# Up-projection pairs in an alternating order, down activations split inside the last pair, and the last norm's weight moved to ScalarE, in a decoder block on one core

## The chip, the core and the metric

The kernel runs on one core of a Trainium2 chip. The metric is the device time of one execution in microseconds; the times given are medians over runs. The program is written against engines by name: TensorE (PE) multiplies, VectorE (DVE), ScalarE (ACT) and GpSimd (POOL) do the rest, SyncE (SP) and GpSimd issue transfers.

## The reference

One decoder block for 512 tokens of 2048 channels in float32: an RWKV-7 head group and a pooling head group that share one input projection, an output projection, then a gated feed-forward part with a causal convolution of width 3, each modulated by `c`, and a last RMS norm with weight `norm_f_g`. What matters here is the last part:

```python
def _conv_ffn(h, w_up, conv_w, conv_b, w_down):
    u = h @ w_up                                   # 2048 -> 2 * 5632
    up = jnp.pad(u, ((0, 0), (CONV_WIDTH - 1, 0), (0, 0)))
    y = conv_b
    for j in range(CONV_WIDTH):
        y = y + conv_w[j] * up[:, j:j + T]
    val, gate = jnp.split(y, 2, axis=-1)
    return (jax.nn.silu(gate) * val) @ w_down      # 5632 -> 2048
...
    mix = jnp.concatenate([y_rwkv, y_pool], axis=-1) @ w_out[l]
    x = x + gt1 * mix
    h = _rmsnorm(x, norm2_g[l]) * (1.0 + sc2) + sh2
    x = x + gt2 * _conv_ffn(h, w_up[l], conv_w[l], conv_b[l], w_down[l])
return _rmsnorm(x, norm_f_g)
```

## The kernel before

Every float32 product is made of three products of halves: a weight tile is cast by ScalarE to a high part (`uhi`, line 850) and DVE subtracts it from the weight to get the low part (`ulo`, line 852); `mm3` (lines 120 to 122) then issues three matmuls for each of the eight tiles of 128 channels. One such `product` is 24 matmuls of 256 columns (128x256 outputs). There are three buffers for `uhi` and `ulo` of the wide kind.

The up-projection runs over 44 pairs `j`; a pair is one tile of 128 value columns and one of 128 gate columns, for both halves of the tokens (`H0`, `H1`, 256 each). It uses the seven-product form for 2x2 blocks instead of eight: the right-hand sides are Y11, Y21, Y22 and sums T1, T2, T3, T4 of them, and the left-hand sides are weights and sums of weights. A pair's two rows of weights, 1 MB each (`row`, line 865), hold `w11`, `w12` in the first and `r1`, `w22` in the second. GpSimd's accumulating transfer (line 972 before) adds other weights from memory onto `r1` once that second row has landed; `r3` is loaded by SP and gets an accumulating transfer of its own (lines 974 and 975). DVE forms `r2 = r1 + w11` (line 996) and `r4 = r2 + w12` (line 1003). The products follow in the order Y11, Y21, T1, T2, Y22, T3, and the pair's last, with `w22` and T4, stands behind the next pair's first product (`last_product`). `finish_pair` then applies the convolution (two DVE passes each, lines 933 and 934, after ScalarE's), SiLU and the product with the value, and stores the activation tile to memory.

Ten pairs, `j < NB`, have their Y11 and Y21 products made earlier, in a time in which T1 to T4 are not yet there (`first_two`), and stored to memory (`early`). These are the stored pairs: in the loop they read that result back and have five products; the others, here the ordinary pairs, have seven. The row buffers of all pairs rotate through four places (`x2_0` to `x2_3`).

The engines' order is not the order of the text: a scheduler places the instructions of each engine within limits, and an engine then runs its list strictly in turn. SP's list of transfers is such a list too.

After the pairs comes the down-projection. `act_pair` loads two activation tiles (`al`), casts and splits them (lines 1040 and 1041 before); `down_four` begins four output tiles in blocks of eight activations. `ada_gate2` makes the second gate: sixteen loads of 1 MB (`wa`) and sixteen DVE dot products (`jk`, line 1027). The down weights have three wide buffers (`wd`) and two in `wd2`. At the end the residual, the rows' sums of squares, and the last norm: `finish` multiplies one tile of 128x256 by the weight and by the row's scale, and stores it.

Ahead of the pairs is the output projection, whose `out_half` splits its weights (`wlo`, line 115) on DVE, and for the last six tiles on DVE and GpSimd in turn.

Of the kernel before, what the change touches and what calls it, by code (L numbers as in the profile page):

```python
# [9 lines left out]
F32 = mybir.dt.float32  # L10
# [6 lines left out]
P = 128  # L17
# [38 lines left out]
def block_kernel(ctx, tc, a, out, stop=None, dbg=None):  # L56
# [67 lines left out]
    def project(ps, src, acts, start=True, stop=True, engs=(V,)):  # L124

        n = len(acts)
        for k0 in range(0, n, WC // P):
            wh, wl = split_weights(src[:, k0 * P : k0 * P + WC], engs[k0 // 4 % len(engs)])
            for kk in range(WC // P):
                k = k0 + kk  # L130
                sl = slice(kk * P, (kk + 1) * P)
                last = mm3(ps, wh[:, sl], wl[:, sl], *acts[k], start=start and k == 0, stop=stop and k == n - 1)
        return last
# [571 lines left out]
    def half(acts, hf):  # L705
        sl = slice(hf * HT, (hf + 1) * HT)
        return [(h[:, sl], l[:, sl]) for h, l in acts]

    def wide(name):

        return rb.tile([P, 4, HT], F32, tag="wide", name=name, bufs=3)
# [57 lines left out]
    for f in range(8):  # L769
        out_done(f, pss[f], 0, T)  # L770

    def out_half(hf, f, engs=(V,)):
        ps = bank()[:, 0:HT]
        project(ps, a["wout"][f, :, :], half(M, hf), engs=engs)
        out_done(f, ps, hf * HT, (hf + 1) * HT)


# [26 lines left out]
    for f in range(8, KT):  # L804
        if f == 9:
            dg = norm_rows(acc[:, H0])
        if f == 10:
            rstd = norm_bcast(dg)
        if f >= 10:
            next(steps, None)  # L810
            if f % 2:
                next(steps, None)
        out_half(1, f, (V, G) if f >= 10 else (V,))

    ea = ctx.enter_context(tc.tile_pool(name="ea", bufs=1, reuse_waits="tile"))
    hctx.close()
# [23 lines left out]
        def done(self):  # L840
            free.append(self.home)

    nsplit = [0]

    def wsplit(src):
        n = src.shape[-1]
        pool, tag = ((ea, "0"), (ea, "1"), (ub, "2"))[nsplit[0] % 3]
        nsplit[0] += 1
        hi = pool.tile([P, 2 * QW], F32R, tag="whi" + tag, name="uhi")
        S.copy(hi[:, 0:n], src)  # L850
        lo = pool.tile([P, 2 * QW], F32R, tag="wlo" + tag, name="ulo")
        V.tensor_tensor(lo[:, 0:n], src, hi[:, 0:n].bitcast(F32), op=ALU.subtract)  # L852
        return hi, lo

    def product(ps, w, Y, start=True):
# [82 lines left out]
    def finish_pair(j, u1, u2):  # L938
# [9 lines left out]
        nc.sync.dma_start(ad[j], yv.t)  # L948
        yv.done()

    pend = None

    def last_product(p):

        j, u1, u2, b, w22, x = p
        product(b, w22, T4, start=False)
        if x is None:
            S.copy(u2[:, H0], b)
        else:
            V.tensor_add(u2[:, H0], x[:, H0], b)  # L960
            x.done()
        finish_pair(j, u1, u2)

    rows = 0
    for j in range(NF):
        w = []
        for i in range(2):
            w.append(row(2 * j + i, rb, f"x2_{(0, 2, 1, 3)[rows % 4]}"))
            rows += 1

        w11, w12, r1, w22 = w[0][:, W1], w[0][:, W2], w[1][:, W1], w[1][:, W2]
        G.dma_start(r1, a["wup"][2 * j + 1, :, W2], accum_op=ALU.add)
        r3 = wide("r3").rearrange("p a b -> p (a b)")
        nc.sync.dma_start(r3, a["wup"][2 * j, :, W1])
        G.dma_start(r3, a["wup"][2 * j + 1, :, W1], accum_op=ALU.add)
        pa = bank()[:, 0:HT]
        cap = Slot("cap")
        if j < NB:
            u1 = Slot("u1")
            nc.sync.dma_start(u1.t, early[j])  # L980
            if pend:
                last_product(pend)
        else:
            product(pa, w11, Y11)
            S.copy(cap[:, H0], pa)
            last_product(pend)
            u1 = Slot("u1")
            pb = bank()[:, 0:HT]
            product(pb, w12, Y21)
            V.tensor_add(u1[:, H0], cap[:, H0], pb)  # L990
        u2 = Slot("u2")
        pc = bank()[:, 0:HT]
        product(pc, r1, T1)
        S.copy(cap[:, H1], pc)
        r2 = wide("r2").rearrange("p a b -> p (a b)")
        V.tensor_add(r2, r1, w11)
        product(pa, r2, T2, start=j < NB)
        if j < NB:
            V.tensor_add(cap[:, H0], u1[:, H1], pa)
        else:  # L1000
            S.copy(cap[:, H0], pa)
        r4 = wide("r4").rearrange("p a b -> p (a b)")
        V.tensor_add(r4, r2, w12)
        product(pc, r4, Y22, start=False)
        V.tensor_add(u1[:, H1], cap[:, H0], pc)
        if j < NB:
            pd = bank()[:, 0:HT]
            product(pd, r3, T3)
            V.tensor_add(u2[:, H1], cap[:, H0], cap[:, H1])
            V.tensor_add(u2[:, H1], u2[:, H1], pd)  # L1010
            pend = (j, u1, u2, pd, w22, cap)
        else:
            product(pa, r3, T3, start=False)
            V.tensor_add(u2[:, H1], cap[:, H1], pa)  # L1014
            cap.done()
            pend = (j, u1, u2, pa, w22, None)
    last_product(pend)


    cb = quad(0, "cb2").rearrange("p a b -> p (a b)")  # L1020
    nc.sync.dma_start(cb, cact[0:1, :].partition_broadcast(P))
# [2 lines left out]
    def ada_gate2(i):  # L1024
        wa = quad(1 + i % 2, "wa2").rearrange("p a b -> p (a b)")
        nc.sync.dma_start(wa, a["ada3"][i, :, :])
        V.scalar_tensor_tensor(jk, wa, 1.0, cb, op0=ALU.mult, op1=ALU.mult, accum_out=mod[:, 80 + i : 81 + i])

    ATAGS = [(rb, "y0"), (rb, "y1"), (rb, "y2"), (rb, "y3")]
    ATAGS += [(ub, f"{t}{g}") for t in ("t1", "t2", "y22", "t3") for g in range(2)] + [(ea, "t40")]  # L1030
    wd2 = ea.tile([P, 2, 2 * QW], F32, tag="t41", name="wd2")

    def act_pair(i):

        pool, tag = ATAGS[i % len(ATAGS)]
        t = pool.tile([P, 2, 2, T], F32R, tag=tag, name="act2")
        for n in range(2):
            s_ = Slot("al")
            nc.sync.dma_start(s_.t, ad[2 * i + n])
            S.copy(t[:, 0, n, :], s_.t)  # L1040
            V.tensor_tensor(t[:, 1, n, :], s_.t, t[:, 0, n, :].bitcast(F32), op=ALU.subtract)
            s_.done()
        return [(t[:, 0, n, :], t[:, 1, n, :]) for n in range(2)]

    nrow = [0]

    def down_row():
        nrow[0] += 1
        if nrow[0] % 5 < 2:
            return wd2[:, nrow[0] % 5, :]  # L1050
        return wide("wd").rearrange("p a b -> p (a b)")

    def down(ps, f, h, acts, blocks=(0, 8, 16)):
        for k0 in blocks:
# [8 lines left out]
    def down_four(h, acts):  # L1063

        pss = [bank() for _ in range(4)]
        for k0 in (0, 8, 16):
            while len(acts) < min(k0 + 8, NJ):
                acts += act_pair((h * NJ + len(acts)) // 2)
            for f in range(4):
                down(pss[f], f, h, acts, (k0,))  # L1070
        return pss

    yd = [tc.dram_tile([P, T], F32, name=f"yd{f}") for f in range(KT)]
    A, A2 = [], []
    for f in range(KT):
        if f == 0:
            pss = down_four(0, A)
        ps = pss[f] if f < 4 else bank()
        if f >= 4:
            down(ps, f, 0, A)  # L1080
        s_ = Slot("yd")
        S.copy(s_.t, ps)
        G.dma_start(yd[f], s_.t)
        s_.done()
        if f == KT - 3:
            A2 += act_pair(NJ // 2) + act_pair(NJ // 2 + 1)
        if f < 8:
            ada_gate2(2 * f)
            ada_gate2(2 * f + 1)
    V.tensor_add(mod[:, 80:96], mod[:, 80:96], cols("b_ada", 80, 96))  # L1090

    def gate(f):
# [14 lines left out]
    def down_half(hf, f):  # L1107
        ps = bank()[:, 0:HT]
        down(ps, f, 1, half(A, hf))
        residual(f, ps, gate(f), acc, hf * HT, (hf + 1) * HT, False)  # L1110

    def finish(hf, k, rstd):
        hs = slice(hf * HT, (hf + 1) * HT)
        V.scalar_tensor_tensor(x2(k, hs), x2(k, hs), col("nf", k), rstd, op0=ALU.mult, op1=ALU.mult)
        nc.sync.dma_start(out[:, k, hs], x2(k, hs))

    for f in range(NWF):
        if f == 0:
            pss = down_four(1, A)
        load_x2(f)  # L1120
        load_x2(f + NWF)
        ps = pss[f] if f < 4 else bank()
        if f >= 4:
            down(ps, f, 1, A)
        residual(f, ps, gate(f), acc, 0, T, f == 0)
    for f in range(NWF, KT):
        down_half(0, f)
    for f in range(NWF, KT):
        n = f - NWF
        if n == 1:  # L1130
            dg = norm_rows(acc[:, H0])
        if n == 2:
            rstd = norm_bcast(dg)
        for k in range(3 * (n - 2), min(3 * (n - 1), KT) if n < 7 else KT):
            if k >= 0:
                finish(0, k, rstd)
        down_half(1, f)
    rstd = norm_bcast(norm_rows(acc[:, H1]))
    for k in range(KT):
        finish(1, k, rstd)  # L1140


def pack(x, c, w_ada, b_ada, norm1_g, w_in, mu_shift, w0, w2, a0, a2, g2, k_k, k_a, r_k, ln_x_w, ln_x_b,
# [95 lines left out]
```

## Time and profile before

| | |
|---|---|
| time, median of 3 runs | 2438.1 us (2434.01 to 2439.13) |
| the profiled execution | 2440.98 us, of which the span is 2439.2 |
| mean granted TensorE clock of it | 0.985 |
| busy: TensorE, DVE, ScalarE, GpSimd | 2295.3 us (94%), 1643.0 (67%), 1039.9 (43%), 139.7 (6%) |
| moved by DMA | 483.06 MB, mean 198 GB/s |

In the rows that follow, a line such as L852 is that of the kernel before, a row "x" is a count, and times are microseconds unless marked ns. "`wrow<-wup`" names the tile written and the tensor read; buffer numbers are left out. A releaser ("<-DVE ulo L852") is the instruction that ended the wait ahead of it. The span is divided into stages: the mixers, the output projection and the second norm to about 1045 us (the output projection's last tiles from about 935 to 985), the stored pairs to 1243, the ordinary pairs to 1917, the down-projection to 2424, then the last norm.

### The profile page before, as it was taken

The numbers are of one execution on the slowest core, as the hardware profiler recorded it, in microseconds if no ns is written. First come the engines' busy times: TensorE is split into PE (matmuls) and PEld (weight loads), VectorE is DVE, ScalarE is ACT, GpSimd is POOL, SyncE is SP. The second block draws the span as 40 slices with busy tenths as digits, with TensorE's granted clock in tenths as the row PEclk, the third lists the DMA queues.
The fourth block names the chain that finished last, engine by engine and source line by source line (L and its number), as shares of the span: only waits on it lengthen the run. The fifth ranks groups of instructions, "written<-read, shape, count | busy, mean of one in ns | idle before, by whom it ended". The sixth has DMA issues, their size and how long they took to land.

```text
span 2439.2 us, 42721 instructions
## 1 busy us (share of the span) xinstructions
PE 2295.3 (94%) x17122; PEld 1986.5 (81%) x17122; DVE 1643.0 (67%) x2636; ACT 1039.9 (43%) x1466; POOL 139.7 (6%) x195
## 2 busy tenths in 40 slices
PE   4889999999999999988899999999999899999997
PEld 3656666667666898987799999999999788888897
DVE  7987777777774466866677777777777762253355
ACT  3234343443433346643345555555555522232242
POOL 0000000000000013110000000000000010010000
PEclk9999999999999999999999999999999999999999
DMA  9975565656672766677777777777676895454365
GB/s 347 343 232 154 171 172 142 168 167 178 166 206 83 245 191 181 235 217 216 218 207 200 196 199 199 201 195 199 195 196 195 282 346 179 121 195 129 112 182 164
DMA packets 214330, 483.06 MB, mean 198 GB/s; under 512 B 73521, under 2 KB 79089, under 8 KB 194673
## 3 DMA queue, kind: packets, MB, share of 16 engines
q1 hardware_dynamic: 195410, 414.77, 52.6%
q0 software_dynamic: 18720, 65.55, 13.3%
q8 instruction: 134, 2.20, 0.4%
q14 instruction: 66, 0.54, 0.1%
HBM read 441.70 MB, written 38.54 MB: 197 GB/s over the span
## 4 chain that ended last, share of the span: by engine, by line
PE 77%; DVE 9%; DMA 7%; issue 4%; ACT 3%; SPq 0%; POOL 0%; DVEq 0%; POOLq 0%; ACTq 0%
PE b L122 18%; PE b L120 18%; PE b L121 18%; PE mm L121 3%; PE mm L120 3%; PE mm L122 3%; DMA wrow<-wup 3%; DVE jk L212 2%; DVE ulo L852 1%; PE pb L537 1%; DMA war<-ada 1%; PE pb L535 1%; DMA wraw<-win 1%; PE pb L528 1%; PE pa L298 1%
## 5 line engine op out<-in xcount | busy, mean ns | idle before, releaser
L122 PE MATMUL b<-t,ulo 128*128 128x256 f32 x1408 | 404.5, 287 | 33.6 <-DVE ulo L852 33.6
L120 PE MATMUL b<-t,uhi 128*128 128x256 f32 x1408 | 402.6, 286 | 3.3 <-DVE u L1014 2.6
L121 PE MATMUL b<-t,uhi 128*128 128x256 f32 x1408 | 401.9, 285 | 0.0
L120 PE MATMUL b<-act,uhi 128*128 128x512 f32 (+1 forms) x880 | 308.5, 351 | 5.9 <-ACT uhi L850 5.9
L122 PE MATMUL b<-act,ulo 128*128 128x512 f32 (+1 forms) x880 | 308.5, 351 | 0.0
L121 PE MATMUL b<-act,uhi 128*128 128x512 f32 (+1 forms) x880 | 308.3, 350 | 0.0
L122 PEld LDWEIGHTS b<-t,ulo 128*128 128x128 f32 x1408 | 272.6, 194 | 37.1 <-DVE ulo L852 37.1
L120 PE MATMUL b<-y,uhi 128*128 128x256 f32 x1056 | 298.0, 282 | 1.3 <-ACT uhi L850 1.3
L122 PE MATMUL b<-y,ulo 128*128 128x256 f32 x1056 | 298.0, 282 | 0.4 <-DVE ulo L852 0.3
L121 PE MATMUL b<-y,uhi 128*128 128x256 f32 x1056 | 297.9, 282 | 0.0
L850 ACT CAST uhi<-wrow 128x1024 fp32r<-128x1024 f32 x176 | 183.7, 1048 | 223.0 <-PE b L121 207.0
L120 PEld LDWEIGHTS b<-t,uhi 128*128 128x128 f32 x1408 | 272.8, 194 | 4.1 <-ACT act L1040 2.8
L852 DVE TENSOR_TENSOR ulo<-wd,uhi 128x1024 fp32r<-128x1024 f32 (+1 forms) x120 | 136.1, 1135 | 205.3 <-ACT uhi L850 202.0
L121 PEld LDWEIGHTS b<-t,uhi 128*128 128x128 f32 x1408 | 272.5, 194 | 0.0
L852 DVE TENSOR_TENSOR ulo<-wrow,uhi 128x1024 fp32r<-128x1024 f32 x176 | 214.7, 1222 | 81.8 <-ACT uhi L850 81.8
L113 ACT CAST whi<-wraw 128x512 fp32r<-128x512 f32 x236 | 145.4, 618 | 286.0 <-PE mm L121 117.2
L850 ACT CAST uhi<-wd 128x1024 fp32r<-128x1024 f32 (+1 forms) x120 | 117.3, 978 | 301.4 <-PE b L121 272.3
L115 DVE TENSOR_TENSOR wlo<-wraw,whi 128x512 fp32r<-128x512 f32 x224 | 156.2, 700 | 108.0 <-ACT whi L113 92.3
L850 ACT CAST uhi<-r 128x1024 fp32r<-128x1024 f32 x132 | 138.5, 1049 | 171.0 <-PE b L121 165.5
L120 PEld LDWEIGHTS b<-y,uhi 128*128 128x128 f32 x1056 | 200.4, 190 | 1.7 <-ACT uhi L850 1.7
L122 PEld LDWEIGHTS b<-y,ulo 128*128 128x128 f32 x1056 | 199.9, 189 | 0.8 <-DVE ulo L852 0.8
L852 DVE TENSOR_TENSOR ulo<-r,uhi 128x1024 fp32r<-128x1024 f32 x132 | 160.9, 1220 | 57.9 <-ACT uhi L850 57.9
(308 smaller groups left out, 4699.3 us busy)
## 6 DMA issues: line engine op xcount, KB each, us to landing
wrow<-wup SPq DMA_DIRECT2D x98, 1024.0 KB, 5.3
wa<-ada SPq DMA_DIRECT2D x48, 1024.0 KB, 7.0
war<-ada SPq DMA_DIRECT2D x192, 256.0 KB, 3.5
wd<-wdn SPq DMA_DIRECT2D x80, 512.0 KB, 4.1
wraw<-win SPq DMA_DIRECT2D x140, 256.0 KB, 4.2
wraw<-wout SPq DMA_DIRECT2D x96, 256.0 KB, 3.6
wrow<-wup POOLq DMA_DIRECT2D x44, 512.0 KB, 5.8
r<-wup SPq DMA_DIRECT2D x44, 512.0 KB, 4.5
```

Source lines behind the costliest of these rows:

```text
L113: S.copy(hi, raw)
L115: eng.tensor_tensor(lo, raw, hi[:, :].bitcast(F32), op=ALU.subtract)
L120: PE.matmul(ps, wh, xh, start=start, stop=False, skip_group_check=more)
L121: PE.matmul(ps, wh, xl, start=False, stop=False, skip_group_check=more)
L122: return PE.matmul(ps, wl, xh, start=False, stop=stop, skip_group_check=more)
L212: V.scalar_tensor_tensor(jk, wa, 1.0, cb, op0=ALU.mult, op1=ALU.mult, accum_out=mod[:, j : j + 1])
L298: PE.matmul(ps, pw[:, i, d * P : (d + 1) * P], zs[i], start=i == 0, stop=i == 1)
L528: PE.transpose(pst[:, i * P : (i + 1) * P], src[:, cl], ident)
L535: PE.matmul(pss[h][:, 0:128], bt[HS[h], cl], ar[HS[h], c, 1, :], start=True, stop=True)
L537: PE.matmul(pss[h][:, 128:384], kt[HS[h], cl], ar[HS[h], c, :, :], start=True, stop=True)
L850: S.copy(hi[:, 0:n], src)
L852: V.tensor_tensor(lo[:, 0:n], src, hi[:, 0:n].bitcast(F32), op=ALU.subtract)
```

## The change

There are four edits. First, the 44 pairs run in the order 10, 0, 11, 1, ..., 19, 9, 20, 21, ..., 43, so that each of the ten stored pairs stands behind an ordinary one. Second, eight activation tiles of the down-projection are loaded and split by calls inside the last pair; the last pair's last product stands behind the first down product; the `ada_gate2` dot products go from output tiles 0 to 7 to tiles 4 to 11, behind the last weight split issued so far; the down weights take three wide buffers and then the two of `wd2`. Third, `out_half` splits all its weights on DVE. Fourth, the last norm's weight is multiplied in by ScalarE tile by tile as the residuals come out; `finish` then multiplies four tiles at a time by the row's scale and stores them with one transfer. For the second half of the tokens GpSimd multiplies the first four tiles, from a copy of the scale that ScalarE makes.

```diff
-    def out_half(hf, f, engs=(V,)):
+    def out_half(hf, f):
...
-        out_half(1, f, (V, G) if f >= 10 else (V,))
+        out_half(1, f)
...
+    def ahead_of_down(j):
+        if j == NF - 1:
+            A.extend(act_pair(len(A) // 2))
...
+    order = [j for n in range(NB) for j in (NB + n, n)] + list(range(2 * NB, NF))
     rows = 0
-    for j in range(NF):
+    for j in order:
...
-            last_product(pend)
+            if pend:
+                last_product(pend)
...                                 (ahead_of_down(j) after Y21, T1, T2 and Y22)
-    last_product(pend)
...
     def down_row():
+        if nrow[0] % 5 > 2:
+            w = wd2[:, nrow[0] % 5 - 3, :]
+        else:
+            w = wide("wd").rearrange("p a b -> p (a b)")
         nrow[0] += 1
-        if nrow[0] % 5 < 2:
-            return wd2[:, nrow[0] % 5, :]
-        return wide("wd").rearrange("p a b -> p (a b)")
+        return w
...
                 down(pss[f], f, h, acts, (k0,))
+                if h == 0 and k0 == 0 and f == 0:
+                    last_product(pend)
...
-        if f < 8:
-            ada_gate2(2 * f)
-            ada_gate2(2 * f + 1)
+        if 4 <= f < 12:
+            with tc.issue_after(lo_of[0].ins):
+                ada_gate2(2 * f - 8)
+                ada_gate2(2 * f - 7)
...
+    def last_residual(f, ps, lo, hi):
+        residual(f, ps, gate(f), acc, lo, hi, f == 0)
+        S.activation(x2(f, slice(lo, hi)), x2(f, slice(lo, hi)), AF.Identity, bias=eps[:, 2:3], scale=col("nf", f))
...
-    def finish(hf, k, rstd):
-        hs = slice(hf * HT, (hf + 1) * HT)
-        V.scalar_tensor_tensor(x2(k, hs), x2(k, hs), col("nf", k), rstd, op0=ALU.mult, op1=ALU.mult)
-        nc.sync.dma_start(out[:, k, hs], x2(k, hs))
+    def finish(hs, q, rstd, eng=V):
+        x = x2q[q][:, :, hs]
+        eng.tensor_tensor(x, x, rstd[:, None, :].to_broadcast([P, 4, HT]), op=ALU.mult)
+        nc.sync.dma_start(out[:, 4 * q : 4 * q + 4, hs], x)
...
-    for k in range(KT):
-        finish(1, k, rstd)
+    rs = Slot("rs")
+    S.copy(rs[:, H0], rstd)
+    finish(H1, 0, rs[:, H0], G)
+    for q in range(1, 4):
+        finish(H1, q, rstd)
```

How the order moves, at three places. SP's transfers in the stage of the stored pairs, before: the first two rows are the second row of a stored pair and the first row of the next.

```order
L865 DMA wrow_13113<-wup 128x2048
L865 DMA wrow_13343<-wup 128x2048
L974 DMA r3_13116<-wup 128x1024
L948 DMA ad11_10662<-yv_12947 128x512
L865 DMA wrow_13345<-wup 128x2048
L865 DMA wrow_13575<-wup 128x2048
L974 DMA r3_13348<-wup 128x1024
```

The same list after the change, where `u1<-early7` belongs to stored pair 7, whose rows are 13743 and 13745; the rows 13919 and 13921 are those of an ordinary pair, 14151 the first of stored pair 8.

```order
L1003 DMA u1_13753<-early7_9927 128x512
L865 DMA wrow_13745<-wup 128x2048
L865 DMA wrow_13919<-wup 128x2048
L997 DMA r3_13748<-wup 128x1024
L948 DMA ad6_10657<-yv_13579 128x512
L865 DMA wrow_14151<-wup 128x2048
L865 DMA wrow_13921<-wup 128x2048
L997 DMA r3_13924<-wup 128x1024
```

Before, a pair's second row always stood ahead of the next pair's first one. Now that holds for stored pairs, and an ordinary pair's second row (13921) stands behind the next stored pair's first one (14151).

DVE's list in the stage of the stored pairs, before. `r2_11970` belongs to the next pair, `r3_11716` and `wrow_11713` (its `w22`) to the present one.

```order
L996 TENSOR_TENSOR r2_11970<-wrow_11889,wrow_11887 128x1024
L934 SCALAR_TENSOR_TENSOR yg_11753<-u2_11587,ncw_10649,yg_11753 128x510
L852 TENSOR_TENSOR ulo_11859<-r3_11716,uhi_11857 128x1024
L946 TENSOR_TENSOR yv_11752<-yv_11752,yg_11753 128x512
L999 TENSOR_TENSOR cap_11720<-u1_11721,b_11719 128x256
L852 TENSOR_TENSOR ulo_11901<-wrow_11713,uhi_11899 128x1024
```

After: `r2_11612` belongs to an ordinary pair (rows 11471 and 11473), `r3_11300` and `wrow_11297` to the stored pair ahead of it.

```order
L1022 TENSOR_TENSOR r2_11612<-wrow_11473,wrow_11471 128x1024
L934 SCALAR_TENSOR_TENSOR yg_11337<-u2_11173,ncw_10649,yg_11337 128x510
L1025 TENSOR_TENSOR cap_11304<-u1_11305,b_11303 128x256
L852 TENSOR_TENSOR ulo_11443<-r3_11300,uhi_11441 128x1024
L946 TENSOR_TENSOR yv_11336<-yv_11336,yg_11337 128x512
L1037 TENSOR_TENSOR u2_11347<-cap_11304 128x256
L852 TENSOR_TENSOR ulo_11483<-wrow_11471,uhi_11481 128x1024
L1032 TENSOR_TENSOR u1_11305<-cap_11304,b_11348 128x256
L852 TENSOR_TENSOR ulo_11512<-wrow_11297,uhi_11510 128x1024
```

The next pair's `r2` add stands ahead of the present pair's `r3` split in both. Now the split of the ordinary pair's Y11 weight (`wrow_11471`) stands between that and the split of the stored pair's `w22`.

DVE's list at the step into the down-projection, before: `u2_20181` is the last pair's, `act2` are activations.

```order
L1041 TENSOR_TENSOR act2_20385<-al_20386,act2_20385 128x512
L1005 TENSOR_TENSOR u1_20150<-cap_20080,b_20182 128x256
L1027 SCALAR_TENSOR_TENSOR jk2_20345,mod_92<-wa2_20800,cb2_20343 128x2048
L1014 TENSOR_TENSOR u2_20181<-cap_20080,b_20079 128x256
L933 SCALAR_TENSOR_TENSOR yv_20332<-u1_20150,vec_67,yv_20332 128x511
```

The same list of DVE after the change:

```order
L962 TENSOR_TENSOR act2_20531<-al_20532,act2_20531 128x512
L852 TENSOR_TENSOR ulo_20367<-wd_20363,uhi_20365 128x1024
L962 TENSOR_TENSOR act2_20301<-al_20302,act2_20301 128x512
L1032 TENSOR_TENSOR u1_20150<-cap_20080,b_20191 128x256
L852 TENSOR_TENSOR ulo_20395<-wrow_20073,uhi_20393 128x1024
L962 TENSOR_TENSOR act2_20301<-al_20306,act2_20301 128x512
L933 SCALAR_TENSOR_TENSOR yv_20422<-u1_20150,vec_67,yv_20422 128x511
L1042 TENSOR_TENSOR u2_20190<-cap_20080,b_20079 128x256
```

The first down weight's split (`wd_20363`) now stands ahead of the last pair's `w22` split (`wrow_20073`) and of its `u2` add, and the dot product is gone from between.

More of the change, by code (lines that the diff above doesn't have):

```diff
@@ L770, in block_kernel @@
         out_done(f, pss[f], 0, T)
-    def out_half(hf, f, engs=(V,)):
+    def out_half(hf, f):
         ps = bank()[:, 0:HT]
-        project(ps, a["wout"][f, :, :], half(M, hf), engs=engs)
+        project(ps, a["wout"][f, :, :], half(M, hf))
         out_done(f, ps, hf * HT, (hf + 1) * HT)
@@ L841, in done @@
             free.append(self.home)
-    nsplit = [0]
+    nsplit, lo_of = [0], [None]
     def wsplit(src):
@@ L851, in wsplit @@
         lo = pool.tile([P, 2 * QW], F32R, tag="wlo" + tag, name="ulo")
-        V.tensor_tensor(lo[:, 0:n], src, hi[:, 0:n].bitcast(F32), op=ALU.subtract)
+        lo_of[0] = V.tensor_tensor(lo[:, 0:n], src, hi[:, 0:n].bitcast(F32), op=ALU.subtract)
         return hi, lo
@@ L949, in finish_pair, with act_pair @@
         yv.done()
+    ATAGS = [(rb, "y0"), (rb, "y1"), (rb, "y2"), (rb, "y3")]
+    ATAGS += [(ub, f"{t}{g}") for t in ("t1", "t2", "y22", "t3") for g in range(2)] + [(ea, "t40")]
+    def act_pair(i):
+        pool, tag = ATAGS[i % len(ATAGS)]
+        t = pool.tile([P, 2, 2, T], F32R, tag=tag, name="act2")
+        for n in range(2):
+            s_ = Slot("al")
+            nc.sync.dma_start(s_.t, ad[2 * i + n])
+            S.copy(t[:, 0, n, :], s_.t)
+            V.tensor_tensor(t[:, 1, n, :], s_.t, t[:, 0, n, :].bitcast(F32), op=ALU.subtract)
+            s_.done()
+        return [(t[:, 0, n, :], t[:, 1, n, :]) for n in range(2)]
+    A = []
+    def ahead_of_down(j):
+        if j == NF - 1:
+            A.extend(act_pair(len(A) // 2))
     pend = None
@@ L990, in block_kernel @@
             V.tensor_add(u1[:, H0], cap[:, H0], pb)
+        ahead_of_down(j)
         u2 = Slot("u2")
@@ L994, in block_kernel @@
         S.copy(cap[:, H1], pc)
+        ahead_of_down(j)
         r2 = wide("r2").rearrange("p a b -> p (a b)")
@@ L1001, in block_kernel @@
             S.copy(cap[:, H0], pa)
+        ahead_of_down(j)
         r4 = wide("r4").rearrange("p a b -> p (a b)")
@@ L1005, in block_kernel @@
         V.tensor_add(u1[:, H1], cap[:, H0], pc)
+        ahead_of_down(j)
         if j < NB:
@@ L1027, in ada_gate2 @@
         V.scalar_tensor_tensor(jk, wa, 1.0, cb, op0=ALU.mult, op1=ALU.mult, accum_out=mod[:, 80 + i : 81 + i])
-    ATAGS = [(rb, "y0"), (rb, "y1"), (rb, "y2"), (rb, "y3")]
-    ATAGS += [(ub, f"{t}{g}") for t in ("t1", "t2", "y22", "t3") for g in range(2)] + [(ea, "t40")]
     wd2 = ea.tile([P, 2, 2 * QW], F32, tag="t41", name="wd2")
[L1033 to L1043, printed above, removed]
     nrow = [0]
     def down_row():
+        if nrow[0] % 5 > 2:
+            w = wd2[:, nrow[0] % 5 - 3, :]
+        else:
+            w = wide("wd").rearrange("p a b -> p (a b)")
         nrow[0] += 1
-        if nrow[0] % 5 < 2:
-            return wd2[:, nrow[0] % 5, :]
-        return wide("wd").rearrange("p a b -> p (a b)")
+        return w
     def down(ps, f, h, acts, blocks=(0, 8, 16)):
@@ L1070, in down_four @@
                 down(pss[f], f, h, acts, (k0,))
+                if h == 0 and k0 == 0 and f == 0:
+                    last_product(pend)
         return pss
     yd = [tc.dram_tile([P, T], F32, name=f"yd{f}") for f in range(KT)]
[L1074 removed]
+    A2 = []
     for f in range(KT):
@@ L1109, in down_half @@
         down(ps, f, 1, half(A, hf))
-        residual(f, ps, gate(f), acc, hf * HT, (hf + 1) * HT, False)
-    def finish(hf, k, rstd):
-        hs = slice(hf * HT, (hf + 1) * HT)
-        V.scalar_tensor_tensor(x2(k, hs), x2(k, hs), col("nf", k), rstd, op0=ALU.mult, op1=ALU.mult)
-        nc.sync.dma_start(out[:, k, hs], x2(k, hs))
+        last_residual(f, ps, hf * HT, (hf + 1) * HT)
+    def last_residual(f, ps, lo, hi):
[5 more added lines that the diff above has]
+        nc.sync.dma_start(out[:, 4 * q : 4 * q + 4, hs], x)
     for f in range(NWF):
@@ L1124, in block_kernel @@
             down(ps, f, 1, A)
-        residual(f, ps, gate(f), acc, 0, T, f == 0)
+        last_residual(f, ps, 0, T)
     for f in range(NWF, KT):
@@ L1133, in block_kernel @@
             rstd = norm_bcast(dg)
-        for k in range(3 * (n - 2), min(3 * (n - 1), KT) if n < 7 else KT):
-            if k >= 0:
-                finish(0, k, rstd)
+        if n >= 3 and n < 7:
+            finish(H0, n - 3, rstd)
         down_half(1, f)
     rstd = norm_bcast(norm_rows(acc[:, H1]))
-    for k in range(KT):
-        finish(1, k, rstd)
+    rs = Slot("rs")
[3 more added lines that the diff above has]
+        finish(H1, q, rstd)
 def pack(x, c, w_ada, b_ada, norm1_g, w_in, mu_shift, w0, w2, a0, a2, g2, k_k, k_a, r_k, ln_x_w, ln_x_b,
```

## The prediction

> **What bounds the kernel now.** The page's first line and its fourth part, the chain that ended last, come first.
>
> ```profile
> span 2439.2 us, 42721 instructions
> PE 77%; DVE 9%; DMA 7%; issue 4%; ACT 3%; SPq 0%; POOL 0%; DVEq 0%; POOLq 0%; ACTq 0%
> ```
>
> TensorE carries the end, so a change counts only where TensorE stands still or runs slow. Second, the table by stage: the up-projection's ten stored pairs, its ordinary pairs, the step into the down-projection, and one stretch inside the down-projection. Columns: length, then busy time (and instructions) of PE, PEld, DVE, ACT, POOL, then clock, DMA share and GB/s.
>
> ```profile
> 1044.61:1243.17 198.56, 164.23 (x1250) 160.18 (x1249) 134.90 (x173) 77.89 (x94) 18.65 (x22) 0.94 0.77 216
> 1255.00:1800.00 545.00, 545.00 (x4582) 545.00 (x4582) 413.48 (x463) 286.77 (x381) 47.41 (x55) 1.00 0.71 199
> 1902.88:1935.00 32.12, 23.60 (x147) 21.31 (x146) 27.22 (x36) 16.20 (x25) 0.00 (x0) 0.84 0.81 275
> 2050.00:2100.00 50.00, 50.00 (x216) 40.40 (x215) 11.31 (x11) 11.58 (x14) 1.89 (x4) 1.00 0.39 114
> ```
>
> In ordinary pairs TensorE never stops: 545/4582 = 0.119 us a matmul, 24 matmuls a product, so 2.85 us a product and 20.0 us a pair of seven. At that pace the stored stage's 1250 matmuls need 148.7 us; it takes 198.6. So **49.9 us** are lost there. Third, who TensorE waits for in that stage (total, times, longest), and the chain between two row loads of it (start, length, what):
>
> ```profile
> PE b L122 <- DVE ulo L852: 24.2, 14, 2.6
> ```
>
> ```profile
> 1196.16 6.32 DMA wrow<-wup
> 1203.04 4.82 DMA wrow<-wup
> 1210.39 0.12 DVE r L996
> 1211.53 0.74 DVE yg L934
> 1212.28 0.79 DVE ulo L852
> 1214.02 0.33 DVE cap L999
> 1215.51 4.72 DMA wrow<-wup
> ```
>
> It is a loop of 19.35 us from row load to row load: the second row lands, GpSimd's accumulating transfer of the other row onto it lands some 7.3 us after its issue at 1203.04, at 1210.39 DVE comes to the end of the wait for it and adds `r2`, and some 5 us of DVE work later the low part of `w22` is split, which frees the buffer for the next second row. A stored pair has only 5 × 2.85 = 14.2 us for TensorE, so the loop sets its pace.
>
> **The change, term one: alternating the pairs.** An ordinary and a stored pair now stand in turn, 12 products, 34.26 us of TensorE for two pairs. Every `r2` add still waits in DVE's order for its accumulate, and each row has its buffer for longer. The transfers' times, issue to landing (minimum/median/maximum), in this order: rows in stored pairs, accumulates in stored pairs, rows in ordinary pairs, accumulates in ordinary pairs, a first row issued 1.8 us behind a second one (1197.97), two rows issued at 1057.8 and 1059.3, where the order happened to be first row, then second (the issue's row stands last), and the accumulate onto that second row.
>
> ```profile
> DMA to landing us min/median/max: 4.9/6.4/7.4
> DMA to landing us min/median/max: 6.7/7.5/8.1
> DMA to landing us min/median/max: 4.7/4.9/6.6
> DMA to landing us min/median/max: 5.4/5.7/6.9
> DMA to landing us min/median/max: 6.9/6.9/6.9
> DMA to landing us min/median/max: 6.7/7.9/9.1
> DMA to landing us min/median/max: 5.9/5.9/5.9
> ...
> L865 SPq DMA_DIRECT2D wrow<-wup x2: 327/327/327, 1057.8 to 1059.3; - x2
> ```
>
> Two loops are left (the early results' loads, the stores of activations and GpSimd's accumulates keep their place within each pair, so no queue gets longer). The second row of a stored pair is still issued ahead of the next first row; it has nearly two pairs' time, and its loop of about 11 us does not bind. The second row of an *ordinary* pair now goes out on SP behind the first row of another pair, as at 1057.8. Its delay is a load of 7.0 (bounds: 6.2, a plain row with little in its way, and 9.1), 0.55 from landing to GpSimd's issue (1202.48 to 1203.04 in the chain), an accumulate of 5.7 (5.4 to 7.5): 13.25, bounds 12.2 and 17.2. I take 7.0 since a row behind a row took 6.9, and the ordinary accumulate since, as at 1068.95, it starts when the rows ahead have landed.
>
> A DVE pass over 128x1024 and ScalarE's cast of a weight (its mean in ns stands behind its busy time):
>
> ```profile
> L780 DVE TENSOR_TENSOR xr<-x,b x6: 1207/1212/1220, 941.5 to 999.5; 128x1024 f32<-128x1024 f32 x6
> L850 ACT CAST uhi<-r 128x1024 fp32r<-128x1024 f32 x132 | 138.5, 1049 | 171.0 <-PE b L121 165.5
> ```
>
> From the ordinary pair's `r2` to its next row issue: `r2`, the rest of the gate's convolution, a capture add and the low part of `r3` on DVE, 1.21 + 0.74 + 0.33 + 1.21 = 3.5; then six products at TensorE's pace (T3 of the stored pair, Y11, T4, Y21, T1, T2) before a weight buffer is free for `w22`, 17.1; its cast and low part, 1.05 + 1.21, of which some 2.2 shows. That is 22.8. With 13.25 the two-pair period is 36.0, so TensorE waits 1.8 a period. What such a gap does to the clock:
>
> ```profile
> 1180.08 0.58 PE L122 MATMUL b<-t,ulo 128*128 128x256 f32 x1 [2.54 <-DVE ulo L852]
> 1180.46 0.41 PE L120 MATMUL b<-t,uhi 128*128 128x256 f32 x1
> 1180.67 0.41 PE L121 MATMUL b<-t,uhi 128*128 128x256 f32 x1
> 1183.45 0.28 PE L122 MATMUL b<-t,ulo 128*128 128x256 f32 x1
> ```
>
> After 2.54 us of standstill the starts lie 0.21 apart for 3.3 us, then 0.12: about 1.4 us more. For a gap of 1.8 I take half of it, 0.7: period 36.7. The Trainium skill, "TensorE: Matmul & The Clock Gate", section "HAM oscillation — how this bites in real kernels", says only gaps over about 3.4 us throttle; by it the period stays 36.0 and this term comes out 7 us better, but the rows show the slow matmuls after 2.54 us. Ten periods lose 10 × (36.7 − 34.26) = 24.4, and I add 3 for filling the loop at the stage's start. **Term one: 49.9 − 27.4 = 22.5 us gained.** At 12.2 without cold matmuls the gain is 39, at 15.5 (9.1 + 0.55 + 5.9) with 1.25 for cold ones it is −6.
>
> **Term two: into the down-projection.** TensorE's waits there, then DVE's rows around the first, then the price of one activation's split on DVE:
>
> ```profile
> PE b L120 <- ACT uhi L850: 5.9, 1, 5.9
> PE b L120 <- DVE u L1014: 2.6, 1, 2.6
> ```
>
> ```profile
> 1914.30 2.28 DVE L1027 SCALAR_TENSOR_TENSOR jk<-wa,cb 128x2048 bf16<-128x2048 f32 x1
> 1916.51 0.41 DVE L1014 TENSOR_TENSOR u<-cap,b 128x256 f32<-128x256 f32 x1
> ```
>
> ```profile
> L1041 DVE TENSOR_TENSOR act<-al,act 128x512 fp32r<-128x512 f32 x13 | 8.7, 685 | 2.6 <-ACT act L1040 2.6
> ```
>
> The last product waited for an add that stood behind a `jk` dot product of 2.28; the first down product waited 5.9 for its weight's split. With about 2 of slow clock (granted 0.84), 10.5 us. Now the first down product (24 matmuls of 512 columns, 50/216 = 0.23 each, 5.5 us) stands ahead of the last product and covers that add, and no `jk` is there. Against it, eight activations must be split inside the last pair: 8 × 0.69 = 5.5 us of DVE in four remaining products, 11.4 us, where DVE is 413/545 = 76% busy; the next pair's two splits and adds, about 4.5, fall away. I leave 2.5 of delay: **8 us gained**, bounds 3 and 10.5. The sixteen `jk` (16 × 2.28 = 36.5 us of DVE, and the 1 MB loads before them on SP's queue) go to later down tiles, where TensorE is 50.00 of 50 and DVE 11.31: nothing. If a weight load behind two such loads were late there, 7 us at most; the loads stood beside weights before as well, without a stop after 1950. The new rotation of the down weight buffers: nothing.
>
> **Term three: the output projection's splits.** TensorE's waits from 935 to 985, GpSimd's twelve splits (shortest, median, longest in ns), DVE's beside them, DVE's in the whole kernel:
>
> ```profile
> PE b L122 <- POOL wlo L115: 2.7, 3, 1.0
> L115 POOL TENSOR_TENSOR wlo<-wraw,whi x12: 1271/1294/1789, 939.2 to 978.1; 128x512 fp32r<-128x512 f32 x12
> L115 DVE TENSOR_TENSOR wlo<-wraw,whi 128x512 fp32r<-128x512 f32 x14 | 12.4, 892 | 5.8 <-ACT whi L113 5.5
> L115 DVE TENSOR_TENSOR wlo<-wraw,whi 128x512 fp32r<-128x512 f32 x224 | 156.2, 700 | 108.0 <-ACT whi L113 92.3
> ```
>
> DVE gets 12 × 0.70 = 8.4 us more, and gets back 14 × 0.19 = 2.7 since its own splits drop from 0.89 to 0.70. The 2.7 us of waits for GpSimd go; a little comes back as waits for DVE. **1.5 us gained**, bounds +4 and −2.
>
> **Term four: the end.** The chain's last row, the DMA row of these stores (us to landing), and the fullest stretch of DMA in the down-projection (last two numbers: share, GB/s):
>
> ```profile
> 2430.70 3.92 DVE x L1114 x10
> out<-x SPq DMA_DIRECT2D x16, 128.0 KB, 1.8
> 1950.00:2000.00 50.00, 50.00 (x218) 40.65 (x217) 34.84 (x33) 11.36 (x14) 2.22 (x4) 1.00 0.91 344
> ```
>
> The multiplies began at 2428.3. Before, a tile left about every 0.5 us, behind its multiply (3.92/10 = 0.39) and SP's issue; the last multiply ended at 2434.6, the last store was issued at 2436.2 and landed at 2437.9. Now ScalarE copies the row scale (about 0.4, an estimate from its cast of four times the columns, 1.05), GpSimd multiplies four tiles; twice its median split is 2.6 (twice the slowest, 3.6), and its store heads SP's queue, at 2428.2 + 0.4 + 2.6 + 0.3 = 2431.5. DVE's three of 1.21 are done at 2432.3 and wait behind it. Then 2.1 MB follow without a break: at 350 GB/s, about what the fullest stretch has, 6.0, and 1.3 (1.8 less a small store's own transfer of 0.5) to the landing, 2438.8. **0.9 us lost**, bounds −0.5 and +3. The weight's passes on ScalarE (busy 11.58 of 50 in such stretches) lie under TensorE's work; the last one, under 1 us, lies beside DVE's and TensorE's sums of squares, and would cost that much if it did not. The Trainium skill, "GPSIMD Engine Reference", section "Specifications", has GpSimd share its memory interface with DVE instructions that read two SBUF inputs; DVE's three read the scale from PSUM, so by it GpSimd stays at 2.6, which agrees with the choice; no run here shows it.
>
> **Sum.** −22.5 − 8 − 1.5 + 0.9 = −31.1 on the profiled execution's 2441.0, giving 2409.9; that execution lay 2.9 above the median 2438.1, so **2407**.
>
> **Rivals.** *TensorE alone sets the pace:* rows come in 6.2 and nothing cools; the loss shrinks to about 7, gain 43 − 0.9 + 9.5, 2386. For it: ordinary pairs never wait at a similar DMA share, 0.71. Chance 0.18. *The reversed rows cost what they cost at 1059:* 15.5, period 39.5, term one −6, total 2435. For it: that is the one place with this order. Against: the pipeline was only filling there. Chance 0.13. *Slower:* the same 9.1, and the accumulate meets the early-result reads and stores of stored pairs at 7.5: 17.2, period 41.2, loss 73, total 2452. It decides from a delay of 16.3 on. Chance 0.12. *The last pair is too full for DVE,* term two gives nothing: 2415, chance 0.07. My forecast keeps 0.50.
>
> **How the numbers follow.** The range reaches from the first rival, 2386, to just under the second, 2434; it leaves out the slower rival and tails. A difference under 0.2% (4.9 us) could not be told from no change in this kernel. Faster: 0.50 + 0.18 + 0.07 and a third of the second rival, 0.79; same 0.06; slower 0.15.
>
> **What would show it.** In the changed profile: the stored stage with waits under 2 us once in two pairs on `ulo` of `r3`; second rows of ordinary pairs landing in about 7.0; no `jk` near the last pair and under 3 us of wait there; no POOL split after 935; stores landing within 3 us of the old time. A two-pair period over 39.3 would make the forecast wrong, and so would waits moving to DVE's own queue in the stage.

## The result, and the profile after

The changed kernel takes 2439.24 us (median of 12 runs, 2433.21 to 2445.28), the kernel before 2438.59 in the same comparison (12 runs, 2432.95 to 2448.64). The ratio is 1.000, with a 95% interval from 0.9986 to 1.0013: no change that can be measured. The forecast was 2407, its range 2386 to 2434.

The page of the changed kernel, first line and the chain that ended last:

```profile
span 2434.2 us, 42678 instructions
PE 73%; DMA 10%; DVE 9%; issue 3%; ACT 3%; SPq 1%; DVEq 0%; POOLq 0%; ACTq 0%
```

TensorE's part of the chain has shrunk and DMA's grown from 7% to 10%. The profiled execution lies 3 us below its median and that of before 2 us above, so the 5 us between their spans are chance; the stages tell more. Their lengths are taken from the trace between five moments: the first product of the up-projection (its first `ulo` matmul), the first product of pair 20 (ahead of it stand pairs 0 to 19, whatever their order), the end of the last pair's Y21, the last down matmul, the end.

| us | to the first up product | early products and pairs 0–19 | pairs 20–43 | down-projection | end |
|---|---|---|---|---|---|
| before | 982.7 | 452.0 | 476.9 | 512.8 | 14.8 |
| changed | 984.2 | 456.7 | 477.1 | 500.8 | 15.5 |

The step into the down-projection gave 12.0 us. Pairs 0 to 19 in the alternating order, which should have given most of it, took 4.7 us longer. The first column varies between 978 and 986 in the executions of this study, also with nothing changed ahead of it but a few splits, so it tells little.

The windows that answer to those shown of before: the alternating pairs, an ordinary stretch, and the step into the down-projection.

```profile
1052.03:1440.86 388.83, 353.63 (x2811) 349.73 (x2809) 275.74 (x331) 176.24 (x226) 34.12 (x39) 0.95 0.72 204
1452.00:1800.00 348.00, 348.00 (x2927) 348.00 (x2926) 265.01 (x296) 183.71 (x244) 30.64 (x35) 1.00 0.71 197
1917.95:1950.00 32.05, 32.02 (x162) 26.97 (x162) 22.00 (x28) 16.92 (x24) 0.00 (x0) 1.00 0.76 244
```

At 348/2927 = 0.119 us a matmul the alternating pairs need 334.2 us and take 388.8: 54.6 us are lost, where 49.9 were lost before and 27.4 were forecast. The losses are no longer in the ten stored pairs alone; they lie over all twenty. TensorE stood still for 35.2 of these (388.83 − 353.63); the other 19.4 are busy time above the 334.2, at a granted clock of 0.95. In the last row TensorE no longer stops. Who TensorE waits for in the alternating pairs (total, times, longest):

```profile
PE b L122 <- DVE ulo L852: 34.3, 13, 4.5
```

Now one period of two pairs, from the timeline. First DVE's rows out of it (start, length, idle time ahead and its end): the `r2` adds of an ordinary pair, a stored pair and the next ordinary pair, and the splits of `w22` between them.

```profile
1155.31 1.22 DVE L1022 TENSOR_TENSOR r<-wrow 128x1024 f32<-128x1024 f32 x1 [4.30 <-DMA wrow<-wup]
...
1160.98 1.22 DVE L852 TENSOR_TENSOR ulo<-wrow,uhi 128x1024 fp32r<-128x1024 f32 x1
...
1175.71 1.22 DVE L1022 TENSOR_TENSOR r<-wrow 128x1024 f32<-128x1024 f32 x1
...
1179.56 1.23 DVE L852 TENSOR_TENSOR ulo<-wrow,uhi 128x1024 fp32r<-128x1024 f32 x1 [0.23 <-ACT uhi L850]
...
1195.21 1.23 DVE L1022 TENSOR_TENSOR r<-wrow 128x1024 f32<-128x1024 f32 x1 [3.69 <-DMA wrow<-wup]
```

SP's row loads of the same stretch (two each), and GpSimd's accumulates:

```profile
1162.22 5.36 SPq L865 DMA_DIRECT2D wrow<-wup  x2
...
1179.36 1.78 SPq L865 DMA_DIRECT2D wrow<-wup  x2
```

```profile
1167.47 0.88 POOL L995 DMA_DIRECT2D wrow<-wup  x1 [15.70 <-DVE r L1030]
...
1189.52 0.88 POOL L995 DMA_DIRECT2D wrow<-wup  x1 [11.02 <-DMA wrow<-wup]
```

And how long these four transfers took: the stored pair's second row (issued at 1162.22), the accumulate onto it (1167.47), the ordinary pair's second row (1180.81), the accumulate onto that (1189.52).

```profile
DMA to landing us min/median/max: 4.7/4.7/4.7
DMA to landing us min/median/max: 8.2/8.2/8.2
DMA to landing us min/median/max: 8.2/8.2/8.2
DMA to landing us min/median/max: 5.6/5.6/5.6
```

Put together they are one ring: a turn of transfers and adds in which each step waits for the one ahead of it. From the ordinary pair's `r2` at 1155.31 DVE comes to the split of the stored pair's `w22`, and the next stored pair's second row goes out at 1162.22: 6.9. Load, hand-over and accumulate take 4.7 + 0.55 + 8.2, and at 1175.71, as soon as that has landed, the stored pair's `r2` runs: 13.5. Then the ordinary pair's `w22` is split, and its successor's second row goes out at 1180.81: 5.1. Load, hand-over and accumulate, 8.2 + 0.55 + 5.6, and the next ordinary `r2` at 1195.21: 14.4. The sum is 39.9 us; over the stage the ordinary pairs' `r2` adds follow each other in 39.8 on average. Before, two pairs, a stored and an ordinary one, took 19.2 + 20.0.

Is the stored pair's add really held by its accumulate? DVE's idle time does not tell it: ahead of the nine stored pairs' adds of this stage DVE stood still for over 1 us only twice (4.25 and 2.79 us). But in eight of the nine the add begins 0.08 to 0.09 us after the accumulate has landed, as in the row at 1175.71, for a landing at 1175.63. In this period a second path through TensorE came out equally long. From the chain of work between 1155 and 1196:

```profile
1158.71 0.58 PE b L122
1159.29 0.21 PE b L120
...
1178.47 1.06 ACT uhi L850
1179.56 1.24 DVE ulo L852
```

After a wait of 3.1 us TensorE's matmuls started 0.21 apart until 1165.04, so its six products took 19.8 us instead of 17.1, and the cast of `w22` behind them made the split wait 0.23 (the row at 1179.56). Three of the nine periods have such a wait, of 0.23 to 0.30. So the ring sets the pace with the slow clock close behind it.

The rows of the two smaller edits. In the output projection from 935 to 985: TensorE's wait and DVE's splits. At the end: the multiplies of GpSimd and DVE (mean ns), then the DMA view from 2418 to 2435, its rate in 40 slices and the four stores.

```profile
PE b L122 <- DVE wlo L115: 4.2, 3, 2.1
```

```profile
L115 DVE TENSOR_TENSOR wlo<-wraw,whi 128x512 fp32r<-128x512 f32 x27 | 18.3, 689 | 10.6 <-ACT whi L113 10.4
```

```profile
L1134 POOL TENSOR_TENSOR x<-x,rs 128x1024 f32<-128x1024 f32 x1 | 2.3, 2342 | 189.2 <-ACT rs L1159 189.2
L1134 DVE TENSOR_TENSOR x<-x,b 128x1024 f32<-128x1024 f32 x3 | 3.5, 1217 | 1.8 <-ACT rs L1159 1.8
```

```profile
GB/s 0 0 0 0 0 0 0 0 0 0 0 0 0 0 0 0 0 0 0 0 0 332 376 388 381 388 386 383 386 388 383 386 386 361 12 0 0 0 0 0
out<-x SPq DMA_DIRECT2D x4, 512.0 KB, 4.1
```

The waits for a GpSimd split are gone and DVE's own splits fell from 0.89 to 0.69 us, while TensorE's waits for them grew from 2.5 to 4.2. At the end GpSimd needed 2.34 us.

### The profile page after: what moved, and what is told of

It reads as the page before. It is cut to its first block, busy times and chain, and to the rows that moved or that the text cites. A ratio compares the mean times of both kernels' runs of the same rounds, so it can differ in the third digit from the quotient of the medians.

```text
span 2434.2 us, 42678 instructions
## 1 busy us (share of the span) xinstructions
PE 2299.5 (94%) x17122; PEld 1990.3 (82%) x17122; DVE 1643.5 (68%) x2623; ACT 1058.0 (43%) x1491; POOL 127.0 (5%) x184
## 4 chain that ended last, share of the span: by engine, by line
PE 73%; DMA 10%; DVE 9%; issue 3%; ACT 3%; SPq 1%; DVEq 0%; POOLq 0%; ACTq 0%
PE b L122 17%; PE b L120 17%; PE b L121 17%; DMA wrow<-wup 7%; PE mm L120 3%; PE mm L121 3%; PE mm L122 3%; DVE jk L212 3%; DVE ulo L852 2%; PE pb L537 1%; PE pb L535 1%; DMA war<-ada 1%; PE pb L528 1%; DMA wraw<-win 1%; DVE wlo L115 1%
## 5 line engine op out<-in xcount | busy, mean ns | idle before, releaser
L115 DVE TENSOR_TENSOR wlo<-wraw,whi 128x512 fp32r<-128x512 f32 x236 | 161.4, 688 | 113.9 <-ACT whi L113 101.3
```

What stands on the lines that cost most here:

```text
L115: eng.tensor_tensor(lo, raw, hi[:, :].bitcast(F32), op=ALU.subtract)
```

## The experiments

The theory, called S below, is the ring just shown: DVE runs its list in turn, each pair's `r2` add waits there for an accumulate, and behind it stands the split that sets free the buffer for another pair's row. Its rivals are named with each run.

**The order alone, and everything but the order.** The first kernel is the one before with

```diff
+    order = [j for n in range(NB) for j in (NB + n, n)] + list(range(2 * NB, NF))
-    for j in range(NF):
+    for j in order:
```

> The kernel before with the alternating order of the pairs and nothing else. Theory S (series): in DVE's list the r2 add of each pair stands ahead of the previous pair's w22 split, so in the alternating order both second rows hang in one ring: r2 of the ordinary pair, 6.9 us, load and accumulate onto the stored pair's second row, 13.0, its r2, 5.1, load and accumulate onto the ordinary pair's second row, 14.6; together 39.7 us for two pairs, as against 19.4 + 20.0 = 39.4 before. It expects 2440 to 2448 us, no gain. Rival F (the forecast's term one held and something else of the change ate it): 2412 to 2420 us.

Measured: 2451.86 us, ratio 1.0053 (1.0040 to 1.0066) to the kernel before. The second is the changed kernel with `order = list(range(NF))`.

> The changed kernel with the pairs in their old order, 0 to 43; the other three edits stay. Theory S: the step into the down-projection gives about 12 us, the output projection's splits and the end cost about 2; 2427 to 2431 us. Rival F: the other three edits cost what the order gained, so this one is slower than before, 2455 us or more.

Measured: 2427.94 us, ratio 0.9959 (0.9945 to 0.9972). So the order costs 11 to 14 us by these medians (2439.24 − 2427.94 in the changed kernel; alone, 2451.86 against 2437.77 of the kernel before in the same comparison) and the other three edits give about 10, which cancel. F falls. S had the order at 2440 to 2448, some 4 us too low: in this execution the two-pair period was 40.3 on average, and pairs 0 to 19 took 461.7 against 452.0, so not all of the cost is shown in the stage.

**Cutting the ring.** In DVE's list each `r2` add is put behind the split of its own pair's T1 weight, which stands behind the previous pair's `w22` split. That is the only edit, but the scheduler moved other entries with it: DVE's `r4` adds and some of its splits, and some of ScalarE's casts. The order of SP's row loads and of GpSimd's accumulates stayed.

```diff
-        V.tensor_add(r2, r1, w11)
+        with tc.issue_after(lo_of[0].ins):
+            V.tensor_add(r2, r1, w11)
```

> The changed kernel with each pair's r2 add put behind the split of that pair's T1 weight in DVE's list, so that it no longer stands ahead of the previous pair's w22 split. Theory S: the ring is cut, each second row is ordered at TensorE's pace, two pairs take 34.3 to 35.5 us instead of 39.7; 2383 to 2400 us. Rival T (the transfers themselves are too slow in this stage, with a DMA share of 0.7 to 0.77): two pairs still take 38 us or more, 2425 to 2440 us.

Measured: 2389.74 us, ratio 0.9802 (0.9789 to 0.9816). The window from 1060 to 1400, in the changed kernel and in this one:

```profile
1060.00:1400.00 340.00, 308.08 (x2443) 304.48 (x2442) 239.08 (x289) 153.73 (x197) 29.80 (x35) 0.95 0.72 205
```

```profile
1060.00:1400.00 340.00, 335.86 (x2800) 333.33 (x2799) 273.30 (x330) 175.96 (x225) 33.74 (x39) 1.00 0.84 232
```

2800 matmuls instead of 2443 in the same time, at a DMA share of 0.84: the transfers were able to, they were asked too late. T falls. Two pairs take 35.0 us.

The same cut in the old order of the pairs:

> The kernel of the old pair order with the other three edits, and each r2 add put behind the split of its pair's T1 weight. Theory S: a stored pair is no longer bound by its ring of 19.4 us. TensorE wants 14.2 us a pair, and the transfers of 19.4 us at a share of 0.77 need 14.9 us of all sixteen engines, so a pair takes 15.5 to 16.5 us: 2395 to 2408 us, slower than the alternating order with the same cut by some 10 us. Rival T: the pair still takes over 18.5 us, 2420 to 2430 us.

Measured: 2395.08 us, ratio 0.9835 (0.9820 to 0.9850). Stored pairs, before and in this kernel:

```profile
1041.00:1230.00 189.00, 155.45 (x1181) 151.79 (x1181) 126.20 (x162) 70.95 (x87) 17.79 (x21) 0.94 0.79 217
```

```profile
1041.00:1230.00 189.00, 179.97 (x1455) 176.86 (x1454) 154.75 (x195) 91.21 (x112) 19.76 (x23) 0.98 0.90 251
```

The same cut works without alternating: 2427.94 without it, 2395.08 with it. With it alternating is worth 5 us, less than the 10 expected: the stored pairs alone bring the DMA share to 0.90, and TensorE waits there for 8.9 us in twelve waits.

**Which link.** The `r2` add is moved behind for the stored pairs only (`if j < NB`), or for the ordinary pairs of the alternating part only (`if NB <= j < 2 * NB`).

> The changed kernel with the r2 add moved behind for the ten stored pairs only, so that the w22 split of an ordinary pair no longer waits for the stored pair's accumulate; the ordinary pairs' r2 adds stay ahead of the stored pairs' w22 splits. Theory S: one link of the ring is cut. Left is the recurrence of the prediction, 22.8 us at TensorE's pace, but with the delay as measured, 8.5 + 0.55 + 5.5 = 14.6: 37.4 us for two pairs, and about 1.3 for slow matmuls after a gap of 3 us: 2418 to 2432 us. Rival T2 (any cut sets the stage free): 2387 to 2397 us.

Measured: 2410.78 us, ratio 0.9883 (0.9867 to 0.9900).

> The changed kernel with the r2 add moved behind for the ten ordinary pairs of the alternating part only; the stored pairs' r2 adds stay ahead of the ordinary pairs' w22 splits. Theory S: from the stored pair's r2, 2.4 us to the split of r3, five products at TensorE's pace, 14.2, cast and split of w22, 2.2, then load and accumulate of the next stored pair's second row, 5.0 + 0.55 + 7.5: 31.9 us, under TensorE's 34.3, so nothing binds: 2385 to 2397 us. Rival (the two links are worth the same): as with the stored pairs' adds, 2418 to 2432 us.

Measured: 2396.70 us, ratio 0.9823 (0.9804 to 0.9841). The same window, with the stored pairs' adds behind, then with the ordinary pairs' adds behind, and TensorE's wait with the stored pairs' adds behind, from 1052 to 1440:

```profile
1060.00:1400.00 340.00, 319.47 (x2634) 315.56 (x2633) 257.30 (x312) 163.92 (x211) 31.40 (x36) 0.99 0.79 221
```

```profile
1060.00:1400.00 340.00, 329.50 (x2741) 326.37 (x2740) 267.50 (x325) 173.21 (x221) 33.16 (x38) 1.00 0.79 229
```

```profile
PE b L122 <- DVE ulo L852: 18.0, 9, 3.4
```

TensorE's wait with the ordinary pairs' adds behind, from 1052 to 1400:

```profile
PE b L122 <- DVE ulo L852: 8.7, 8, 2.6
```

The two links are not worth the same, as S had it, and both rivals fall. With the ordinary pairs' adds behind S expected no wait at all; 8.7 us are left, and the time is at the upper end of its range. With the stored pairs' adds behind, the period is 37.0 us, against 37.4 from the prediction's own recurrence with the measured delay. The time came out 7 us below the range, largely because I had added 1.3 us a period for a slow clock, which nine waits of 2.0 us on average hardly caused (0.99 granted).

**The order of the rows.** SP's row loads of the first twenty pairs strictly pair by pair; DVE's list as in the changed kernel.

```diff
+            if i == 0 and 0 < rows < 4 * NB:
+                with tc.issue_after(row_load[0].ins):
+                    w.append(row(2 * j, rb, tag))
```

> The changed kernel with the row loads of the first twenty pairs issued strictly pair by pair on SP, so that an ordinary pair's second row goes out ahead of the next stored pair's first one; DVE's order stays. Theory S: the ring stays, its one load is 5.0 instead of 8.5 us, and its accumulate meets the row behind it, 7.5 instead of 5.5: 38.2 us for two pairs instead of 39.7, 2418 to 2432 us. Rival (the order of the rows is the cause of the whole miss): two pairs in 35 to 36 us, 2390 to 2405 us.

Measured: 2418.26 us, ratio 0.9922 (0.9896 to 0.9949), and the window:

```profile
1060.00:1400.00 340.00, 319.64 (x2570) 316.35 (x2569) 251.71 (x304) 161.14 (x207) 31.41 (x36) 0.96 0.76 215
```

The period is 37.8 us (38.2 expected). An ordinary pair's second row now landed in 4.9 to 5.0 us (issued at 1169.42, 1207.02) instead of 8.2, in 4.9 to 6.3 over the stage, and the accumulate behind it in 7.2 to 7.9 instead of 5.6. So the place behind another row costs some 2 us of period, and it is not the whole miss.

**A better version.** The cut for the first twenty pairs of the order only:

> The changed kernel with each r2 add behind the split of its pair's T1 weight for the first twenty pairs of the order only; pairs 20 to 43 as they were. With the add behind in all pairs, pairs 20 to 43 took 480.3 us against 477.1. Theory S with that cost avoided: 2383 to 2390 us. Rival (the 3 us have another cause): the same as with all pairs, 2389 to 2393 us.

Measured: 2392.18 us, ratio 0.9799 (0.9784 to 0.9813): no gain over all pairs, the rival was right. DVE's row and TensorE's wait, at the border, show why:

```profile
1391.05 1.23 DVE L1026 TENSOR_TENSOR r<-wrow 128x1024 f32<-128x1024 f32 x1 [6.05 <-issue]
```

```profile
PE b L122 <- DVE ulo L852: 4.0, 1, 4.0
```

Pair 20's add, left in its old place, waits 6.05 us for its accumulate, and the split of the pair ahead waits behind it: the old fault once more, in one place. With the cut for two pairs more (`j < 2 * NB + 2`):

> The changed kernel with the r2 add behind for the alternating twenty pairs and pairs 20 and 21. With twenty alone, the unmoved r2 of pair 20 stood ahead of the split that pair 9 waited for, DVE waited 6.05 us for its accumulate and TensorE 4.0. Theory S: that wait goes, 2385 to 2390 us. Rival: some other pair takes it over, 2390 to 2394 us.

Measured: 2387.63 us, ratio 0.9783 (0.9769 to 0.9796), the fastest with the one beside it; TensorE in the window:

```profile
1060.00:1400.00 340.00, 336.00 (x2802) 333.51 (x2802) 274.74 (x332) 175.97 (x225) 33.20 (x38) 1.00 0.85 232
```

> The same with the row loads of the first twenty pairs strictly pair by pair on SP. Theory S: with the ring cut a second row's landing no longer sets the pace, so a load of 5.0 instead of 8.5 us moves nothing: within 4 us of the kernel beside it. Rival T (the loads still count): 5 to 10 us faster than it.

Measured: 2387.09 us, ratio 0.9787 (0.9774 to 0.9800): with the ring cut the order of the rows moves nothing. T is not needed to explain anything here.

## Why the prediction was wrong, step by step

- **Term one failed, at the sentence that the stored pair's loop "of about 11 us does not bind".** Two things were wrong in it. Its transfers took 13.4 in the period shown (12.3 to 15.0 over the stage): the accumulate took 8.2 us, 6.0 to 9.3 over the stage, with the next first row going out at about the same moment. The 11 stands in the prediction without a sum; 4.9 + 0.55 + 5.7 gives it, with the ordinary pairs' accumulate, though the stored pairs' row with its 7.5 stood there too. And it was judged by itself. The stored pair's `r2` add waits in DVE's list ahead of the ordinary pair's `w22` split, so its delay is a link of the other loop. I had counted from the ordinary `r2` to the next row 22.8 us "at TensorE's pace"; it was 6.9 + 13.5 + 5.1 = 25.5, of which DVE waited 0.23 for TensorE, by way of the cast. The run with only the stored pairs' adds behind shows that the rest of the recurrence held: 37.0 for 37.4. Its clock was higher too (0.99 for 0.95), so how the 2.8 us of period divide between the cut link and the slow matmuls that went with it stays open.
- **The ordinary second row's load was taken at 7.0 and was 7.5 to 9.0**, mostly over 8; the accumulate on it, taken at 5.7, was 5.4 to 6.2. The rival of the reversed rows, with 9.1, came to a period of 39.5, next to the measured 39.8, but by a wrong count: its load was a little too long and the second link was missing from it.
- **The slow clock was charged too little**: 0.7 us a period for gaps of 1.8. In the changed kernel the stage holds 9.8 periods; the 35.2 us of standstill are 3.6 a period, and the 19.4 of busy time above TensorE's pace are 2.0. Nine waits of 2.0 us on average left the granted clock at 0.99 (only the stored pairs' adds behind); thirteen of 2.6 us left it at 0.95 (the changed kernel). The Trainium skill, "TensorE: Matmul & The Clock Gate", section "HAM oscillation — how this bites in real kernels", puts the limit at about 3.4 us. The first, with a longest wait of 3.4, agrees; the second does not, since the wait of 3.1 us ahead of 1158.71 was followed by 6 us of slow matmuls.
- **Term two was right and too small**: 12.0 us instead of 8. The delay of 2.5 that I left for DVE did not come; TensorE is busy 32.02 of 32.05 us there, and the dot products cost nothing where they went (1987 to 2099, while TensorE was busy 150.00 of 150 us from 1950 to 2100).
- **Term three agrees**: the last six tiles took 41.4 us up to the first up product instead of 42.7, 1.3 gained against 1.5. Single executions scatter as much: without the alternating order, with the same splits, it was 39.9.
- **Term four was right**: 0.6 lost against 0.9. GpSimd took 2.34 us, not 2.6, beside DVE multiplies of 1.22 that were not stretched. The Trainium skill, "GPSIMD Engine Reference", section "Specifications", names contention with DVE instructions that have two SBUF inputs, which these had not; the trace agrees. The kernel before has the other case: DVE's splits, with two such inputs, took 0.89 us beside GpSimd's and 0.69 without them.
- With term one at +5 to +14 us, as the stages and the medians have it, instead of −22.5, and the other terms at −12.0 − 1.3 + 0.6, the sum lands between −8 and +1; the medians say 0.7, which cannot be told from nothing. That gains and losses came out so nearly equal is chance.

That the pieces of the medians (11 to 14 for the order) are larger than the stage's own 5 to 10 stays open within the spread of single executions.

## What to carry to other kernels

When a wait sits in the middle of an engine's list, ask what stands behind it: an add that waits for a transfer, placed ahead of the split that frees the buffer for the next transfer, makes a ring of transfers, and reordering the work only changes its length. Loops over the same in-order engine are not judged one by one; follow one whole turn through every list before calling a loop slack. Here one edit to the order of DVE's list, moving `r2` behind the work that does not need it, was worth 50 us, where the rearrangement of 44 pairs by itself cost 11 to 14.

## What the runs showed of the hardware that was not expected

In the alternating pairs a 512 KB accumulate took 5.4 to 6.2 us when the rows ahead of it had landed and 6.0 to 9.3 when a 1 MB row went out about the same moment; a 1 MB row took 4.7 to 6.3 as second row of a stored pair, with no other row issued within 3 us of it; of two rows issued 1.1 to 1.5 us apart the first took 5.8 to 7.6 and the second 7.5 to 9.0. And the last stores ran faster than the 350 GB/s that I took from the fullest stretch: the four of 512 KB each moved at 376 to 388 GB/s in all slices between the first and the last two.
